# A layer of a hybrid decoder trunk: the second norm's parts as two streams, the residual rows on GpSimd's queue, the channel mixer's conditioning later

## The chip, the cores and the metric

The kernel runs on one core of a Trainium2 chip. The metric is the device time of one execution in microseconds; a shorter time is better. Times come from three runs of the kernel before, and one further execution was taken with the hardware profiler. TensorE (PE) does the matrix products, VectorE (DVE), ScalarE (ACT) and GpSimd (POOL) the elementwise work; SyncE (SP), ACT and POOL also issue DMA transfers, each in the order of its own instruction queue.

## The reference

One layer (depth 1) is applied to a prompt of 1024 tokens and to 8 sample groups of 8 tokens with the same weights, all in float32, with 1024 features:

```python
sh, sc, gt = ada_mod(c, w_ada_mix, b_ada_mix)          # silu(c) @ w + b, in three parts
h = rms_norm(x, norm_mix) * (1 + sc) + sh
pr, pp, pg = split(h @ w_in)
o_r = rwkv7_branch(pr, ...)                            # 512 columns, a scan over the tokens
o_p = pool_branch(pp, ...)                             # 512 columns, windowed means
g_r, g_p = split(sigmoid(pg))
merged = g_r * (o_r @ w_br_rwkv) + g_p * (o_p @ w_br_pool)
x = x + gt * (merged @ w_out)
sh, sc, gt = ada_mod(c, w_ada_mlp, b_ada_mlp)
h = rms_norm(x, norm_mlp) * (1 + sc) + sh
x = x + gt * (square(relu(h @ w_ff1)) @ w_ff2)         # hidden width 4096
y = rms_norm(x, norm_final)
```

The states of the branches are outputs too. The change touches the five lines from `merged` to the second `h`, and the way in which every `rms_norm` spreads its row of reciprocal roots.

## The kernel before

**Layout.** Features lie on the 128 partitions, tokens along a row: x is eight tiles of 128 x 1088 (1024 prompt and 64 sample tokens). Tokens are worked in three chunks of 364, 362 and 362; the first two, 726 tokens, are called part 0, the third part 1.

**Products.** A float32 product is made of three passes in a reduced type: hi by hi, hi by lo and lo by hi (`mm3`, L171 to L174), where hi is the rounded value and lo the rest. A weight tile of 128 x 512 is loaded by SP (L164), rounded by ACT (L167, `whi`), and its rest is made by DVE or, for every other tile, by POOL (L168, `wlo`). PSUM has four banks with the tag mm, two with w and two with wc; a bank comes free when its result has been read.

**Order.** PE's order is written out by `Pace.run` (L87): one stream of jobs (products) runs on, and generators (here `norm2` and `ada`) put their few matmuls between, after a given model time or when a condition holds. The scheduler of the tile framework orders the other engines. Every engine, and each DMA queue with it, works strictly in the order of its list.

**The stretch of the change** is `phase2` (L1222). It begins behind the jobs `op_job`, which multiply the pool branch's product into a gate row and save that row to DRAM (`d_th`, L1218 and L1220). Then:

- `or_job(m)`, eight jobs of 36 matmuls: two gate rows are loaded into tiles `t` and `u` (four buffers with the tag t) on ACT's queue (L1244, L1245); DVE multiplies the first with the RWKV branch's product (L1246); POOL adds the second, the *merge* (L1250); ACT and DVE split the sum into hi and lo (L1253, L1254).
- `x_load` (L1264): the eight rows of x, 544 KB each, come on ACT's queue into buffers of the tag hx (L1268).
- `out_job(m, i)`: 24 or 48 matmuls with `w_out` for part i, then the residual (L1433 on DVE; for the sample tokens L1436 on DVE into `rs` and L1438 on POOL).
- `norm2` (L1278), one generator: it waits for the whole conditioning, then for part 0 squares the rows (ACT, L1290), adds them (DVE, L1292), sums over partitions on PE (`stats`), makes the reciprocal roots (`rms`, L281: root L286, reciprocal L287, a copy that repeats each value 128 times L289, transposes on PE L155, ACT L302), modulates the eight rows (DVE L1303, L1305, L1307; ACT L1304, L1309; POOL L1310); and then all of it for part 1.
- `ada` (L1232): the conditioning of the channel mixer, 24 loads `hid` of 512 KB on SP (L249) and 48 narrow matmuls, in three groups: shift, scale and gate.
- `ff1_job` and `ff2_jobs`: the two products of the channel mixer. The first job for part i starts only when norm part i is done.

## Time and profile before

| what | value |
| --- | --- |
| median of 3 runs | 1761.83 us (1758.38 to 1764.14) |
| the profiled execution's own time | 1760.32 us |
| its span, first to last instruction | 1758.5 us |
| PE busy | 1688.9 us, 96% |
| DVE, ACT, POOL busy | 846.8, 546.0, 242.9 us |
| mean granted TensorE clock | 0.984 |
| stretch 786 to 857 us (merge jobs): PE busy, DMA share | 64.33 of 71.00 us, 0.90 |
| stretch 857 to 930 us (output, part 0) | 73.00 of 73.00 us, 0.44 |
| stretch 930 to 985 us (output, part 1, and norm) | 50.00 of 55.00 us, 0.28 |

A row of a timeline reads: start in us, length in us, engine, line, operation, output <- inputs and shapes, and in brackets the time that the engine stood idle before it, with what ended that time. A row of the chain of waits has the start, the length and the work that was waited for. A group's row has the count behind an x, then busy time, mean ns of one, and idle time before. DMA rows have the count, KB each and the median time from issue to landing.

### The profile page before, as it was taken

Reading aid. Unit: us, or ns where it says so; the run is one execution under the profiler, and the core shown is the slowest. Engines: PE = TensorE matmul, PEld = TensorE weight load, DVE = VectorE, ACT = ScalarE, POOL = GpSimd, SP = SyncE. Lnnn points to the kernel's source line nnn. Section 1 sums busy time; section 2 is a strip of 40 time slices with the busy share of each in tenths; the row PEclk is TensorE's granted clock in tenths of the full one; section 3 lists DMA queues with packets and bytes.
Section 4 is the critical chain, followed back from the end, with each engine's and each line's share of the span. In section 5 each row is a group of like instructions: output and inputs, shape, how many; then the busy total and the mean of one; then the engine's idle time right before and its main releaser. Section 6 shows DMA issues by size and latency. Waiting matters only on the chain.

```text
span 1758.5 us, 32538 instructions
## 1 busy us (share of the span) xinstructions
PE 1688.9 (96%) x13705; PEld 1582.7 (90%) x13705; DVE 846.8 (48%) x1546; ACT 546.0 (31%) x1100; POOL 242.9 (14%) x315
## 2 busy tenths in 40 slices
PE   5999999999999999998999999999999999999997
PEld 2989879887887898897889999999999999999996
DVE  5577475646663654344436643333333343323356
ACT  4443343334333433221224521213121222212132
POOL 0110111000000000003313511111111111111111
PEclk9999999999999999998999999999999999999999
DMA  8233314232413332849742211111111111111112
GB/s 336 83 126 119 124 65 138 83 104 88 131 42 127 97 120 72 315 156 356 257 150 78 85 61 42 49 43 43 48 42 48 44 43 48 42 49 43 43 42 103
DMA packets 80084, 179.61 MB, mean 102 GB/s; under 512 B 16481, under 2 KB 23137, under 8 KB 79937
## 3 DMA queue, kind: packets, MB, share of 16 engines
q1 hardware_dynamic: 72128, 156.66, 26.0%
q10 hardware_dynamic: 7664, 20.42, 3.4%
q8 instruction: 108, 1.77, 0.4%
q0 software_dynamic: 144, 0.44, 0.1%
q14 instruction: 40, 0.32, 0.1%
HBM read 138.64 MB, written 38.84 MB: 101 GB/s over the span
## 4 chain that ended last, share of the span: by engine, by line
PE 86%; DVE 5%; DMA 4%; ACT 2%; issue 1%; SPq 0%; DVEq 0%; ACTq 0%; POOL 0%
PE mm L148 58%; PE w L148 24%; PE wc L148 3%; DMA smp<-in_xT 1%; PE w L155 1%; DMA wt<-d_x 1%; DMA wraw<-in_w_in 1%; DVE wlo L168 1%; DMA d_th<-px 0%; DMA hx<-in_xT 0%; DMA t<-d_th 0%; DVE ma L1305 0%; DMA aw<-in_w_ada_mix 0%; DVE hx L1423 0%; DVE t L1303 0%
## 5 line engine op out<-in xcount | busy, mean ns | idle before, releaser
L148 PE MATMUL mm<-hx,whi 128*128 128x362 f32 (+2 forms) x2608 | 684.6, 344 | 9.0 <-DVE t L1246 6.5
L148 PEld LDWEIGHTS mm<-hx,whi 128*128 128x128 f32 x2608 | 459.0, 192 | 47.6 <-issue 28.4
L148 PE MATMUL mm<-hx,wlo 128*128 128x362 f32 (+3 forms) x1304 | 430.1, 330 | 1.8 <-DVE wlo L168 1.8
L167 ACT ACTIVATE whi<-wraw 128x512 fp32r<-128x512 f32 x246 | 155.0, 630 | 537.4 <-PE w L148 365.3
L148 PE MATMUL mm<-ma,whi 128*128 128x364 f32 (+1 forms) x1280 | 318.8, 330 | 0.0
L148 PEld LDWEIGHTS mm<-hx,wlo 128*128 128x128 f32 x1304 | 250.5, 192 | 2.3 <-DVE wlo L168 2.1
L148 PEld LDWEIGHTS mm<-ma,whi 128*128 128x128 f32 x1280 | 227.0, 189 | 6.7 <-issue 5.0
L168 DVE TENSOR_TENSOR wlo<-wraw,whi 128x512 fp32r<-128x512 f32 x157 | 111.9, 713 | 210.6 <-ACT whi L167 210.0
L148 PE MATMUL mm<-ma,wlo 128*128 128x364 f32 (+1 forms) x640 | 210.7, 329 | 0.0
L168 POOL TENSOR_TENSOR wlo<-wraw,whi 128x512 fp32r<-128x512 f32 x89 | 117.3, 1318 | 666.4 <-ACT whi L167 666.2
L1433 DVE SCALAR_TENSOR_TENSOR hx<-mm,aq,hx 128x364 f32<-128x364 f32 (+4 forms) x136 | 74.7, 587 | 206.4 <-PE mm L148 206.3
L148 PE MATMUL w<-mb,whi 128*128 128x362 f32 x640 | 159.0, 330 | 0.6 <-DVE rs L1436 0.6
L148 PEld LDWEIGHTS mm<-ma,wlo 128*128 128x128 f32 x640 | 120.9, 189 | 0.0
L148 PEld LDWEIGHTS w<-mb,whi 128*128 128x128 f32 x640 | 114.0, 191 | 0.8 <-issue 0.8
L1327 DVE TENSOR_TENSOR ft<-ft 128x362 f32<-128x362 f32 (+1 forms) x96 | 53.0, 576 | 127.4 <-ACT ft L1326 127.0
L148 PE MATMUL w<-mb,wlo 128*128 128x362 f32 x320 | 105.4, 329 | 1.3 <-DVE wlo L168 1.3
L148 PE MATMUL w<-hx,whi 128*128 128x362 f32 x416 | 103.5, 330 | 0.1
L148 PE MATMUL mm<-hid,whi 128*128 128x364 f32 (+4 forms) x304 | 75.3, 330 | 0.0
L148 PEld LDWEIGHTS w<-hx,whi 128*128 128x128 f32 x416 | 73.4, 190 | 1.2 <-issue 0.8
L1326 ACT ACTIVATE ft<-mm 128x364 f32<-128x364 f32 x64 | 29.3, 474 | 128.4 <-PE mm L148 128.3
L148 PE MATMUL w<-hx,wlo 128*128 128x362 f32 x208 | 67.8, 326 | 0.0
L148 PEld LDWEIGHTS w<-mb,wlo 128*128 128x128 f32 x320 | 61.1, 191 | 1.7 <-DVE wlo L168 1.7
(301 smaller groups left out, 2074.5 us busy)
## 6 DMA issues: line engine op xcount, KB each, us to landing
wraw<-in_w_ff SPq DMA_DIRECT2D x134, 256.0 KB, 2.6
wraw<-in_w_in SPq DMA_DIRECT2D x68, 256.0 KB, 3.0
hid<-in_w_ada_mlp SPq DMA_DIRECT2D x24, 512.0 KB, 5.1
d_th<-px SPq DMA_DIRECT2D x22, 544.0 KB, 3.1
wt<-d_x SPq DMA_DIRECT2D x20, 544.0 KB, 4.3
t<-d_th ACTq DMA_DIRECT2D x16, 544.0 KB, 6.7
aw<-in_w_ada_mix SPq DMA_DIRECT2D x16, 512.0 KB, 7.1
wraw<-in_w_out SPq DMA_DIRECT2D x32, 256.0 KB, 2.7
```

The source lines that it names most:

```text
L148: return self.nc.tensor.matmul(out, lhsT, rhs, **kw)
L155: self.nc.tensor.transpose(out, in_, ident)
L167: nc.scalar.activation(hi, raw, AF.Copy)
L168: (nc.gpsimd if n % 2 and n >= self.solo else nc.vector).tensor_tensor(lo, raw, hi.bitcast(F32), op=ALU.subtract)
L1326: nc.scalar.activation(t[:, :n], ps[:, :n], AF.Relu)
L1327: nc.vector.tensor_tensor(t[:, :n], t[:, :n], t[:, :n], op=ALU.mult)
L1433: nc.vector.scalar_tensor_tensor(x[:, c0:c0 + m], ps[:, :m], gt[:, 0:1], x[:, c0:c0 + m], op0=ALU.mult, op1=ALU.add)
```

## The change

- **x loads.** `x_load` goes. Each `or_job` ends with a one-column copy on POOL from its merged row into a buffer for x (`behind`), and a load of one row of x into that buffer on POOL's queue. The copy makes the load stand behind the merge.
- **Conditioning.** `ada` starts when the fifth or-job's place in the order is reached (`("or", 8)` is set by job 4). Its first four tiles are tied to merged rows by the same copy. Its third group, the gates, waits until norm part 1 is done, and no longer holds up the norm.
- **Norm.** `norm2(i)` is one generator for each part. The squares and sums of a part no longer wait for the conditioning, and those of part 1 no longer for part 0's modulation; they have an own sum (`acc2`) and use the tiles `ft`. Part 1's modulation waits for part 0's.
- **`rms`.** The copy that repeats each reciprocal 128 times goes; PE's transposes read the single column as a broadcast.

```diff
@@ -278,21 +278,22 @@
             m = len(blocks) if first and i == 0 else 1
             self.mm(po[:, i:i + m], t[:, b:b + 128], self.kc("one0")[:, :m], start=first and i == 0, stop=last and i == len(blocks) - 1)
 
-    def rms(self, po, col, blocks, out, pool):
+    def rms(self, po, col, blocks, out):
 
         nc = self.nc
         k = len(blocks)
         r = self.cp.tile([P, 16], F32, tag="rt", bufs=2, name=self.nm("rt"))[:, :k]
         nc.scalar.activation(r, po[:, col:col + k], AF.Sqrt, bias=self.eps[:, 0:1], scale=1.0 / D)
         nc.vector.reciprocal(r, r)
-        R = self.row(pool, "R", 1, w=9 * 128).rearrange("p (b j) -> p b j", j=128)
-        nc.vector.tensor_copy(R[:, :k, :], r.unsqueeze(2).to_broadcast([P, k, 128]))
         yield 2000
         for i in range(0, k, 4):
             m = min(4, k - i)
             ps = self.ps("wc")
             for j in range(m):
-                self.tr(ps[:, j * 128:(j + 1) * 128], R[:, i + j, :], self.kc("ident"))
+                self.tr(ps[:, j * 128:(j + 1) * 128], r[:, i + j:i + j + 1].to_broadcast([P, 128]), self.kc("ident"))
+            self.rps = ps
+            if out is None:
+                return
             for j in range(m):
                 if j + 1 < m and blocks[i + j + 1] == blocks[i + j] + 128:
                     continue
@@ -394,7 +395,7 @@
                 nc.vector.scalar_tensor_tensor(lo[:, pr], h, sh, hi[:, pr].bitcast(F32), op0=ALU.add, op1=ALU.subtract)
                 nc.vector.tensor_tensor(lo[:, sa], smp[:, kb], hi[:, sa].bitcast(F32), op=ALU.subtract)
 
-        self.pace.run(iter(()), [part(0, (0, 3500, 0, 0), 1000), self.rms(po, 0, blocks, rb, st)])
+        self.pace.run(iter(()), [part(0, (0, 3500, 0, 0), 1000), self.rms(po, 0, blocks, rb)])
         load(1)
 
         def rest():
@@ -1229,11 +1230,26 @@
         orr = self.orr
         mg = [[], []]
 
+        def behind(x):
+
+            nc.gpsimd.tensor_copy(x[:, 0:1], self.mark[:, 0:1])
+            return x
+
         def ada():
-            asb = self.row(p, "R", 1, w=9 * 128)[:, :512]
+            asb = p.tile([P, 512], F32, name="asb2")
+            yield lambda: ("or", 8) in self.done
+            first = 4 * [behind]
+
+            def tile():
+                t = self.row(p, "hid", 4)[:, :1024]
+                return first.pop()(t) if first else t
+
             for g in range(3):
-                yield from self.ada_part("w_ada_mlp", g, lambda: self.row(p, "hid", 4)[:, :1024], asb, self.aq, "b_mlp", (8 * g, 8 * g + 4), 7000, 3000, 15000 if g == 0 else 0)
-            self.done.add("ada")
+                if g == 2:
+
+                    self.done.add("ada")
+                    yield lambda: ("h2", 1) in self.done
+                yield from self.ada_part("w_ada_mlp", g, tile, asb, self.aq, "b_mlp", (8 * g, 8 * g + 4), 6500, 2500, 9000 if g == 0 else 0)
 
         def or_job(m):
             S = {}
@@ -1254,6 +1270,10 @@
                     nc.vector.tensor_tensor(lo[i], t[:, s], hi[i].bitcast(F32), op=ALU.subtract)
                 mg[0].append(hi)
                 mg[1].append(lo)
+                self.mark = t
+                self.xr.append(HX(F32))
+                nc.gpsimd.dma_start(behind(self.xr[m]), io["xT"][m])
+                self.done.add(("or", m + 4))
 
             return Job([io["w_br"][m][:, 0:512]], begin, after=after, xs=lambda: orr, tags=TG)
 
@@ -1261,12 +1281,7 @@
         g2 = self.cp.tile([P, 8, 9], F32, name="g2")
         self.xr = []
 
-        def x_load():
-            nc.vector.tensor_scalar(gt, self.am[:, 16:24, :], 0.5, None, op0=ALU.mult)
-            for m in range(8):
-                self.xr.append(HX(F32))
-                nc.scalar.dma_start(self.xr[m], io["xT"][m])
-            yield
+        nc.vector.tensor_scalar(gt, self.am[:, 16:24, :], 0.5, None, op0=ALU.mult)
 
         def out_job(m, i):
             ch = (CH[:2], CH[2:])[i]
@@ -1275,41 +1290,48 @@
 
         fh, fl = [[None, None] for _ in range(8)], [[None, None] for _ in range(8)]
 
-        def norm2():
+        def norm2(i):
+            a, b = ((0, CUT), (CUT, NT))[i]
+            bl = [x for c0, n in (CH[:2], CH[2:])[i] for x in self.blocks(c0 - a, n)]
+            if i:
+                acc, sq = p.tile([P, NT - CUT], F32, name="acc2"), lambda: p.tile([P, 364], F32, tag="ft", bufs=2, name=self.nm("ft"))[:, :NT - CUT]
+            else:
+                acc, sq = T()[:, :CUT], lambda: T()[:, :CUT]
+            for m in range(8):
+                yield lambda: ("out", m, i) in self.done
+                t = sq() if m else acc
+                nc.scalar.activation(t, self.xr[m][:, a:b], AF.Square)
+                if 0 < m < 7:
+                    nc.vector.tensor_tensor(acc, acc, t, op=ALU.add)
+                if m > 5:
+                    yield 3500
+                    po = self.ps("wc") if m == 6 else po
+                    self.stats(po, acc if m == 6 else t, bl, m == 6, m == 7)
             yield lambda: "ada" in self.done
-            self.mod_scale(g2, self.aq, "norm_mlp")
-            rb = T()
-            for i, ch in enumerate((CH[:2], CH[2:])):
-                a, b = ch[0][0], ch[-1][0] + ch[-1][1]
-                bl = [x for c0, n in ch for x in self.blocks(c0, n)]
-                po = self.ps("wc")
-                acc = T()
-                for m in range(8):
-                    yield lambda: ("out", m, i) in self.done
-                    t = T() if m else acc
-                    nc.scalar.activation(t[:, a:b], self.xr[m][:, a:b], AF.Square)
-                    if 0 < m < 7:
-                        nc.vector.tensor_tensor(acc[:, a:b], acc[:, a:b], t[:, a:b], op=ALU.add)
-                    if m > 5:
-                        yield 3500
-                        self.stats(po, acc if m == 6 else t, bl, m == 6, m == 7)
-                yield from self.rms(po, 0, bl, rb, p)
-                for kb in range(8):
...
-                self.done.add(("h2", i))
+            if i:
+                r = acc
+            else:
+                self.mod_scale(g2, self.aq, "norm_mlp")
+                r = T()[:, :CUT]
+            yield from self.rms(po, 0, bl, r)
+            if i:
+                yield lambda: ("h2", 0) in self.done
+            for kb in range(8):
...
+            self.done.add(("h2", i))
 
         hid = {}
 
@@ -1348,7 +1370,6 @@
         order = []
         for m in range(8):
             order += U(or_job(m))
-        order += [(x_load, 0)]
         for i in range(2):
             for m in range(8):
                 order += U(out_job(m, i))
@@ -1366,7 +1387,7 @@
                 if j == 0 and grp:
                     for j2 in ff2_jobs(grp - 1):
                         order += U(j2)
-        self.pace.run(self.stream(None, order), [norm2(), ada()])
+        self.pace.run(self.stream(None, order), [norm2(0), norm2(1), ada()])
 
 
         w = []
@@ -1413,7 +1434,7 @@
                     if m > 5:
                         yield 2500
                         self.stats(po, acc if m == 6 else t, bl, m == 6, m == 7)
-                yield from self.rms(po, 0, bl, rb[:, c0:c0 + n], p)
+                yield from self.rms(po, 0, bl, rb[:, c0:c0 + n])
                 for m in (7, 6, 0, 1, 2, 3, 4, 5):
                     x = self.xr[m][:, c0:c0 + n]
                     if m > 5 and ci == 2:
```

In the two places marked in `norm2`, the loop over the eight rows is the same before and after (it reads `r` in place of a slice of `rb`).

The change moves instructions at three places that matter here. First, ACT's list at the start of `phase2`, before: `hx<-in_xT` are the x loads, `t_8646` and `t_8647` the gate rows of the first or-job.

```order
L167 ACTIVATE whi_8618<-wraw_8616 128x512
L1268 DMA hx_9175<-in_xT 128x1088
L1035 ACTIVATE hx_8549<-wt_7132 128x576
L1268 DMA hx_9177<-in_xT 128x1088
L1268 DMA hx_9179<-in_xT 128x1088
L1268 DMA hx_9181<-in_xT 128x1088
L1268 DMA hx_9183<-in_xT 128x1088
L1268 DMA hx_9185<-in_xT 128x1088
L167 ACTIVATE whi_8624<-wraw_8622 128x512
L1268 DMA hx_9187<-in_xT 128x1088
L1268 DMA hx_9189<-in_xT 128x1088
L167 ACTIVATE whi_8630<-wraw_8628 128x512
```

The same place of ACT's list in the changed program, up to the gate rows of the second or-job:

```order
L167 ACTIVATE whi_8617<-wraw_8615 128x512
L1036 ACTIVATE hx_8547<-wt_7130 128x576
L167 ACTIVATE whi_8623<-wraw_8621 128x512
L167 ACTIVATE whi_8629<-wraw_8627 128x512
L1260 DMA t_8642<-d_th_90 128x1088
L1261 DMA t_8643<-d_th_98 128x1088
L167 ACTIVATE whi_8635<-wraw_8633 128x512
L1260 DMA t_8706<-d_th_91 128x1088
L1261 DMA t_8707<-d_th_99 128x1088
```

The eight x loads no longer stand ahead of the gate rows on ACT. Second, POOL's list over the first or-jobs in the changed program; before, the merges and the `wlo` rows stand here alone.

```order
L1266 TENSOR_TENSOR t_8642<-t_8642,t_8643 128x1088
L1235 COPY hx_8703<-t_8642 128x1
L1275 DMA hx_8703<-in_xT 128x1088
L1266 TENSOR_TENSOR t_8706<-t_8706,t_8707 128x1088
L168 TENSOR_TENSOR wlo_8752<-wraw_8749,whi_8751 128x512
L1235 COPY hx_8767<-t_8706 128x1
L1275 DMA hx_8767<-in_xT 128x1088
```

Each merge is now followed by its copy and one x load. Third, DVE's list in the norm, before: from the fourth row's residual of part 1 (`hx_9181`) over modulation rows (`t`, `ma`), to the fifth row's (`hx_9183`).

```order
L1307 TENSOR_TENSOR t_9997<-hx_9181,t_9756 128x726
L1305 SCALAR_TENSOR_TENSOR ma_9975<-t_9976,aq,ma_9974 128x726
L1433 SCALAR_TENSOR_TENSOR hx_9181<-w_9967,gt_8614,hx_9181 128x298
L1303 SCALAR_TENSOR_TENSOR t_10013<-hx_9183,g_8615,t_9756 128x726
L1436 TENSOR_TENSOR rs_10024<-w_9967,gt_8614 128x64
L168 TENSOR_TENSOR wlo_9989<-wraw_9986,whi_9988 128x512
L1303 SCALAR_TENSOR_TENSOR t_10039<-hx_9185,g_8615,t_9756 128x726
L1433 SCALAR_TENSOR_TENSOR hx_9183<-w_10027,gt_8614,hx_9183 128x298
```

The same place in the changed program, where `acc_8640` is the sum of part 1's squares and `hx_8895` and `hx_8959` are the fourth and fifth row:

```order
L1329 TENSOR_TENSOR t_9961<-hx_8895,t_9830 128x726
L1327 SCALAR_TENSOR_TENSOR ma_9931<-t_9932,aq,ma_9930 128x726
L168 TENSOR_TENSOR wlo_9972<-wraw_9969,whi_9971 128x512
L1325 SCALAR_TENSOR_TENSOR t_9983<-hx_8959,g_8613,t_9830 128x726
L1305 TENSOR_TENSOR acc_8640<-acc_8640,ft_9950 128x362
L1454 SCALAR_TENSOR_TENSOR hx_8895<-w_9946,gt_8612,hx_8895 128x298
L1457 TENSOR_TENSOR rs_10000<-w_9946,gt_8612 128x64
L1325 SCALAR_TENSOR_TENSOR t_10009<-hx_9030,g_8613,t_9830 128x726
```

An add of squares stands between modulation rows, and the weight rest (`wlo`) ahead of the fourth row's residual instead of behind it.

More of the change, by code (lines that the diff above doesn't have):

```diff
@@ L1276, in phase2 @@
         fh, fl = [[None, None] for _ in range(8)], [[None, None] for _ in range(8)]
-        def norm2():
-            yield lambda: "ada" in self.done
-            self.mod_scale(g2, self.aq, "norm_mlp")
-            rb = T()
-            for i, ch in enumerate((CH[:2], CH[2:])):
-                a, b = ch[0][0], ch[-1][0] + ch[-1][1]
-                bl = [x for c0, n in ch for x in self.blocks(c0, n)]
-                po = self.ps("wc")
-                acc = T()
-                for m in range(8):
-                    yield lambda: ("out", m, i) in self.done
-                    t = T() if m else acc
-                    nc.scalar.activation(t[:, a:b], self.xr[m][:, a:b], AF.Square)
-                    if 0 < m < 7:
-                        nc.vector.tensor_tensor(acc[:, a:b], acc[:, a:b], t[:, a:b], op=ALU.add)
-                    if m > 5:
-                        yield 3500
-                        self.stats(po, acc if m == 6 else t, bl, m == 6, m == 7)
-                yield from self.rms(po, 0, bl, rb, p)
-                for kb in range(8):
-                    hi, lo = fh[kb][i], fl[kb][i] = MG(i), MG(i)
-                    h = T()[:, a:b]
-                    x, r, sh = self.xr[kb][:, a:b], rb[:, a:b], self.aq[:, kb, 0:1]
-                    if i == 0 and kb % 4 < 3:
-                        nc.vector.scalar_tensor_tensor(h, x, g2[:, kb, 0:1], r, op0=ALU.mult, op1=ALU.mult)
-                        nc.scalar.activation(hi, h, AF.Identity, bias=sh)
-                        nc.vector.scalar_tensor_tensor(lo, h, sh, hi.bitcast(F32), op0=ALU.add, op1=ALU.subtract)
-                    else:
-                        nc.vector.tensor_tensor(h, x, r, op=ALU.mult)
-                        self.modulate(h, h, g2, self.aq, kb, a, b - a, a)
-                        nc.scalar.activation(hi, h, AF.Copy)
-                        (nc.gpsimd if kb % 4 == 3 else nc.vector).tensor_tensor(lo, h, hi.bitcast(F32), op=ALU.subtract)
-                    yield 1000
-                self.done.add(("h2", i))
@@ new lines, in norm2 @@
+        def norm2(i):
[15 more added lines that the diff above has]
+                    self.stats(po, acc if m == 6 else t, bl, m == 6, m == 7)
+            yield lambda: "ada" in self.done
+            if i:
[7 more added lines that the diff above has]
+            for kb in range(8):
+                hi, lo = fh[kb][i], fl[kb][i] = MG(i), MG(i)
+                h = T()[:, a:b]
+                x, sh = self.xr[kb][:, a:b], self.aq[:, kb, 0:1]
+                if i == 0 and kb % 4 < 3:
+                    nc.vector.scalar_tensor_tensor(h, x, g2[:, kb, 0:1], r, op0=ALU.mult, op1=ALU.mult)
+                    nc.scalar.activation(hi, h, AF.Identity, bias=sh)
+                    nc.vector.scalar_tensor_tensor(lo, h, sh, hi.bitcast(F32), op0=ALU.add, op1=ALU.subtract)
+                else:
+                    nc.vector.tensor_tensor(h, x, r, op=ALU.mult)
+                    self.modulate(h, h, g2, self.aq, kb, a, b - a, a)
+                    nc.scalar.activation(hi, h, AF.Copy)
+                    (nc.gpsimd if kb % 4 == 3 else nc.vector).tensor_tensor(lo, h, hi.bitcast(F32), op=ALU.subtract)
+                yield 1000
+            self.done.add(("h2", i))
```

## The prediction

> **What bounds the kernel now.** I read the totals first, then PE's own waits in time order, then the chain of waits and the clock around each stop. The page's first lines:
>
> ```profile
> span 1758.5 us, 32538 instructions
> PE 1688.9 (96%) x13705; PEld 1582.7 (90%) x13705; DVE 846.8 (48%) x1546; ACT 546.0 (31%) x1100; POOL 242.9 (14%) x315
> ```
>
> TensorE is the bound, so only its stops and its slow stretches can be won. The change touches the merge, the output product and the second norm (about 786 to 985 us). In PE's timeline there I find three stops:
>
> ```profile
> 811.89 0.95 PE L148 MATMUL mm<-hx,whi 128*128 128x364 f32 x2 [6.48 <-DVE t L1246]
> 955.61 0.57 PE L148 MATMUL w<-mb,whi 128*128 128x362 f32 x2 [0.56 <-DVE rs L1436]
> 957.53 0.43 PE L148 MATMUL w<-mb,wlo 128*128 128x362 f32 x1 [1.35 <-DVE wlo L168]
> 974.51 0.94 PE L148 MATMUL wc<-kct,t 128*128 128x3 f32 x6 [3.09 <-DVE t L1292]
> ```
>
> The bracket is PE's idle time and who ended it. Each stop is followed by a stretch at a lower clock; the view of stretches (length, busy time of PE, PEld, DVE, ACT, POOL, then PE's granted clock, DMA share, GB/s):
>
> ```profile
> 812.00:818.00 6.00, 6.00 (x20) 6.00 (x21) 2.30 (x6) 1.09 (x2) 2.50 (x1) 0.50 1.04 401
> 957.50:961.50 4.00, 3.97 (x14) 3.97 (x15) 4.00 (x7) 2.49 (x4) 1.59 (x3) 0.57 0.23 70
> 974.50:979.00 4.50, 4.49 (x19) 4.49 (x20) 0.56 (x1) 0.79 (x2) 1.27 (x1) 0.62 0.34 113
> 985.00:1190.00 205.00, 205.00 (x1241) 205.00 (x1240) 85.31 (x152) 55.78 (x111) 44.34 (x54) 1.00 0.16 52
> ```
>
> The last row shows PE without a stop at clock 1.00, so each slow stretch is charged to the stop ahead of it: length times (1 - clock). Stop A: 6.48 + 6.0 x 0.50 = 9.5 us. Stop B: 0.56 + 1.35 + 4.0 x 0.43 = 3.6. Stop C: 3.09 + 4.5 x 0.38 = 4.8. That is 17.9 us, the most that the change can win here.
>
> **Stop A: the x loads leave ACT's queue.** The chain of waits around A, in order of time (start, length):
>
> ```profile
> 789.39 7.11 DMA hx<-in_xT
> 796.58 7.69 DMA d_th<-px
> 804.40 6.72 DMA t<-d_th
> ```
>
> Before, a save of the gate product cannot be issued until one of the x loads has landed; the first t load waits for that save, because it writes the save's old buffer; and VectorE's gating, which frees the PSUM bank that PE wants, waits for t. SyncE's waits and ACT's row say the same, and VectorE's row shows that the data of the last save were there early:
>
> ```profile
> SPq L1220 <- DMA hx<-in_xT: 6.3, 1, 6.3
> 804.37 0.63 ACT L167 ACTIVATE whi<-wraw 128x512 fp32r<-128x512 f32 x1 [10.28 <-DMA d_th<-px]
> 792.58 1.52 DVE L1218 SCALAR_TENSOR_TENSOR px<-px,mm 128x364 f32<-128x364 f32 x3 [1.79 <-PE mm L148]
> ```
>
> The product is complete at 792.58 + 1.52 = 794.1. Landing times (KB, median us), the first two rows of the stretch 786 to 805, the last of the whole page:
>
> ```profile
> hx<-in_xT ACTq DMA_DIRECT2D x8, 544.0 KB, 8.9
> d_th<-px SPq DMA_DIRECT2D x2, 544.0 KB, 6.8
> d_th<-px SPq DMA_DIRECT2D x22, 544.0 KB, 3.1
> ```
>
> In the changed program no x load stands on ACT, and the first one on POOL stands behind the first merge. So the save is issued at 794.2 and lands at 797.3 (3.1) or at latest 801.0 (6.8). One weight copy (0.63) is ahead of the t load, which takes from 3.1 (the same size with the x loads away) to 6.72: t is there between 801 and 804.6, in the worst case at 808.4. Gating to PE's start took 811.89 - 811.21, the end of the t load plus 0.1: 0.7 to 0.8. PE wants the bank at 811.89 - 6.48 = 805.4. In the middle cases the bank is free by then; in the worst one 809.2, 3.8 us late, with 3.8 / 6.48 x 3.0 = 1.8 of slow clock. So A gives between 9.5 - 5.6 = 3.9 and 9.5. I take 9.5: the eight loads that made these transfers slow are gone from that stretch.
>
> **Where the x loads go.** They stand on POOL, each behind one merge and a one-column copy that ties it to that merge. POOL's groups in the merge stage, and its rows near the start, the only DMAs it issues before:
>
> ```profile
> L168 POOL TENSOR_TENSOR wlo<-wraw,whi 128x512 fp32r<-128x512 f32 x22 | 30.0, 1364 | 102.1 <-ACT whi L167 102.0
> L1250 POOL TENSOR_TENSOR t<-t,t 128x1088 f32<-128x1088 f32 x8 | 21.4, 2673 | 28.0 <-DMA t<-d_th 16.6 <-PE mm L148 7.2 <-DVE t L1246 3.0
> L427 POOL COPY px<-sst 128x8 f32<-128x8 f32 x2 | 0.9, 460 | 5.6 <-DMA sst<-in_sst 5.6
> 1.99 0.54 POOL L1115 DMA_DIRECT2D kct<-in_kc  x1
> kct<-in_kc POOLq DMA_DIRECT2D x1, 315.5 KB, 6.6
> 856.80 5.96 PE mm L148 x36
> ```
>
> One merge job is 36 matmuls of PE, 5.96 us. POOL's share of a job: merge 2.67, half a weight remainder 0.68, one and a half copies at 0.46 = 0.69, issue 0.54: 4.58 of 5.96. It fits with 1.38 to spare, so I price it at nothing; the cover is that margin, and an issue that holds POOL for more than 0.54 + 1.38 = 1.92 us makes it late, eight times. The upper bound for an issue is the landing itself, 6.6. No issue of POOL's in this trace stands beside a busy VectorE, so the price is not shown here.
>
> The Trainium skill, "SBUF — State Buffer", section "SBUF: two separate sides", speaks against the change at this place: a DMA issued by GpSimd needs descriptors that GpSimd writes, and a VectorE instruction in a two-port mode locks it out; it gives about 620 ns alone and 3100 ns beside such an instruction. By that figure, an estimate from that page, the loss would be 8 x (3.1 - 1.92) = 9.4 us and the time about 1757; no run so far shows it, and it stands below as a rival priced from rows.
>
> The residual reads x only in the output stage, after the last merge job, so an x load has tens of us to land.
>
> **The mixer's conditioning.** Its 24 loads of 512 KB stay on SyncE, but now begin behind the fourth or so merge; the last third, the gates, is computed during the first product of the channel mixer.
>
> ```profile
> hid<-in_w_ada_mlp SPq DMA_DIRECT2D x24, 512.0 KB, 5.1
> ```
>
> The same matmuls run, elsewhere. The one tight place is the second pair of tiles: by the order it is issued about 1.4 us before the last merge job ends, and PE wants it about 5.0 after. 5.1 - 6.4 leaves 1.3 us of slack at the median; a landing of 8.9, like the x loads', would cost 2.5. I charge 0.5 (0 to 2.5). The gates are ready 66 matmuls (11 us at 5.96 us per 36) before the second product begins: nothing.
>
> **Stops B and C: the second norm as two streams.** VectorE's timeline, from the start of the norm's first part to the end of C:
>
> ```profile
> 940.49 0.56 DVE L289 COPY R<-rt 128x768 f32<-128x768 f32 x1
> ...
> 944.83 2.75 DVE L1303 SCALAR_TENSOR_TENSOR t<-hx,g,t 128x726 f32<-128x726 f32 x3 [1.62 <-ACT t L302]
> ...
> 955.25 0.21 DVE L1436 TENSOR_TENSOR rs<-w,gt 128x64 f32<-128x64 f32 x1
> 955.39 2.09 DVE L168 TENSOR_TENSOR wlo<-wraw,whi 128x512 fp32r<-128x512 f32 x1
> 957.40 1.02 DVE L1303 SCALAR_TENSOR_TENSOR t<-hx,g,t 128x726 f32<-128x726 f32 x1
> ...
> 963.27 0.90 DVE L1307 TENSOR_TENSOR t<-hx,t 128x726 f32<-128x726 f32 x1
> 964.10 0.52 DVE L1433 SCALAR_TENSOR_TENSOR hx<-w,gt,hx 128x298 f32<-128x298 f32 x1
> 964.54 0.21 DVE L1436 TENSOR_TENSOR rs<-w,gt 128x64 f32<-128x64 f32 x1
> 964.67 0.96 DVE L1305 SCALAR_TENSOR_TENSOR ma<-t,aq,ma 128x726 fp32r<-128x726 f32 x1
> 965.76 0.69 DVE L168 TENSOR_TENSOR wlo<-wraw,whi 128x512 fp32r<-128x512 f32 x1
> ...
> 967.56 0.53 DVE L1292 TENSOR_TENSOR t<-t,t 128x362 f32<-128x362 f32 x1
> ...
> 971.78 2.67 DVE L1292 TENSOR_TENSOR t<-t,t 128x362 f32<-128x362 f32 x3
> ```
>
> VectorE is the late engine: it modulates part 0, serves part 1's residuals, and only then adds part 1's squares, whose last three (971.78 + 2.67 = 974.45) release C. The change adds no work here; it moves. (1) Part 0's transposes stand 6 matmuls earlier (1.0 us), and the 0.56 copy ahead of them goes, so the modulation starts 0.6 to 1.0 us sooner against PE; I take 0.8. (2) Two of part 1's adds now stand ahead of the fourth row's gating (rs), and the weight remainder that made B's 1.35 stands two operations ahead of it. From the modulation's start to that rs the new list is 2.75 + 1.02 + 3 x 0.96 + 0.90 + 2 x (0.69 + 0.53 + 0.52 + 0.21) = 11.45, less about 0.07 by which each of 13 starts before its predecessor's end (964.10 + 0.52 against 964.54, 964.54 + 0.21 against 964.67): 10.5. Operations here also run long, as 2.09 against 0.69 shows, so 10.5 to 11.7. PE wanted the bank at 955.61 - 0.56 = 955.05, 10.2 after 944.83; now 11.0. Stall 0 to 0.7, I take 0.3. The next remainder, still behind two modulations, I put at 0.7 late (0 to 1.4, B's own size being the bound). (3) The last add stands right behind the last-but-one residual, not behind three others: 3.09 goes to between 0 and 3.09 less the two adds that no longer follow (1.1), 2.0; I take 0.8. Idle left: 1.8 of 5.0. The clock lost there was 3.4; at the same share per idle us it would be 1.2, but B's 1.91 us of idle alone drew 1.7, so I keep 1.6. B and C give 8.4 - 3.4 = 5.0, between 0 and 8.4.
>
> The Trainium skill, "TensorE: Matmul & The Clock Gate", Part 1, puts the slow clock only after an idle window of about 3.4 us. The rows above disagree: 0.57 for 4.0 us after 1.91 us of idle in two pieces. The measurement decides; by the rule the 1.6 would not be lost, and the forecast would be 1745.9.
>
> **The copy of the reciprocal, elsewhere.** It goes from all norms; only the last one lies on the path to the end:
>
> ```profile
> 1749.65 0.30 DVE R L289
> ```
>
> This row of the chain of waits is the 0.3 that I count. The first norm's copy lies behind input loads: nothing. PE's transposes now read one column broadcast; no row shows such a read. The load as it is:
>
> ```profile
> L155 PEld LDWEIGHTS wc<-kct,R x27: 138/142/231, 24.6 to 1750.1; 128*128 128x128 f32 x27
> ```
>
> If it took twice or half as long (27 x 0.14), that would be +3.8 or -1.9 at most; it overlaps the matmul before it, so I take 0.
>
> **Sum.** -9.5 (A) - 5.0 (B, C) - 0.3 + 0.5 = -14.3. Against this execution's own 1760.32 us: 1746.0. The median of the runs is 1.5 above that execution, so 1747.5; I say 1747.
>
> **Rivals.**
> 1. *Only A goes.* VectorE's work in the norm is the same, and B and C merely change their place: -9.5 - 0.3 + 0.5 = -9.3, 1752.5. For it: VectorE is busy without gap from 944.83 on. Against: the adds that release C are moved ahead.
> 2. *All three go* and the conditioning costs nothing: -17.9 - 0.3, 1743.6. Against: the budget of 10.5 to 11.7 against 11.0.
> 3. *POOL's issues wait for VectorE* (the mechanism that the skill's page tells). An issue that is held for two VectorE operations in a row of 1.0 to 1.3 us takes 0.54 + 2.6 = 3.1: 8 x (3.1 - 1.92) = 9.4 lost, -4.9, 1757. Held for one it takes 1.8 and costs nothing.
> 4. *A stays:* the save turns out to wait for another transfer. Then -5.0 - 0.3 + 0.5 = -4.8, 1757. Against: the row that names the x load.
> 5. *Slower:* each issue holds POOL until its transfer has landed, 6.6 us, so POOL sets the merge stage: 8 x (6.6 - 1.92) = 37 lost, +23, about 1785. It decides from 1.92 + 14.3 / 8 = 3.7 us per issue. Against: at 1.99 the issue took 0.54 while its transfer took 6.6.
>
> **How the numbers follow.** My forecast 0.46, rival 1 0.18, rival 2 0.12, rival 3 0.09, rival 4 0.08, rival 5 or another mishap as dear 0.07. Range 1740 to 1758: all three stops with the transposes' gain below, rivals 3 and 4 above. The forecast's own range is 1742 to 1752. 0.3% is 5.3 us, about what a measurement of this kernel tells from no change. Forecast and rivals 1 and 2 are faster (0.76); rivals 3 and 4 lie on the bound, 1757 against 1756.5, a third of them faster (0.05): faster 0.81, same 0.12, slower 0.07.
>
> **What would show it.** In the new profile: no stop of PE at the second merge job, and the merge stage at clock 1.00 (A); the save issued within 1 us of its product; x loads on POOL with issues under 1.9 us; PE's wait on the square adds under 1 us and under 2 us together with B's. I am wrong if POOL's merges start late with the t loads landed, if PE waits for conditioning tiles, or if the waits on VectorE add up to 5 us as before.

## The result, and the profile after

The changed kernel took 1755.55 us (median of 18 runs, 1750.53 to 1759.69) against 1764.6 us for the kernel before (median of 18 runs beside it, 1758.38 to 1771.96): ratio 0.9949, interval 0.9936 to 0.9963, 9 us faster. The forecast was 1747, 14.3 us faster.

The two profiled executions show less: spans of 1758.5 and 1757.5 us. They already differ by 4 us ahead of the change, as this PE row at one and the same place of the program shows, first of the kernel before, then of the changed one (start, length, work, idle time and its end):

```profile
702.80 0.60 PE L148 MATMUL mm<-hx,whi 128*128 128x362 f32 x2 [2.03 <-ACT px L464]
```

```profile
706.97 0.60 PE L148 MATMUL mm<-hx,whi 128*128 128x362 f32 x2 [2.03 <-ACT px L465]
```

In the fourteen profiles of this study that row stands between 701.71 and 709.46 us, with nearly the same work ahead of it. So the profiles are compared below from this common point to the third norm's first sums, also in PE's timeline:

```profile
1732.94 0.83 PE L148 MATMUL wc<-kct,t 128*128 128x3 f32 x6 [0.76 <-DVE t L1412]
```

```profile
1731.64 0.83 PE L148 MATMUL wc<-kct,t 128*128 128x3 f32 x6 [0.79 <-DVE t L1433]
```

That is 1030.1 us before and 1024.7 after, 5.5 us less. PE's stops of the changed kernel in the stretch of the change, the answer to the three stops of before:

```profile
846.79 1.05 PE L148 MATMUL wc<-hid,sT 128*32 128x512 f32 x4 [2.04 <-DMA hid<-in_w_ada_mlp]
856.83 1.05 PE L148 MATMUL wc<-hid,sT 128*32 128x512 f32 x4 [1.35 <-DMA hid<-in_w_ada_mlp]
951.48 0.57 PE L148 MATMUL w<-mb,whi 128*128 128x362 f32 x2 [2.07 <-DVE rs L1457]
960.12 0.57 PE L148 MATMUL w<-mb,whi 128*128 128x362 f32 x2 [0.40 <-ACT t L334]
961.51 0.43 PE L148 MATMUL w<-mb,wlo 128*128 128x362 f32 x1 [0.82 <-DVE wlo L168]
975.40 0.54 PE L155 MATMUL wc<-kct,rt 128*128 128x128 f32 x3 [0.38 <-DVE rt L287]
```

Stop A, 6.48 us at the second merge job, is gone; two stops on the conditioning's tiles have come, 31 and 41 us later by the distance from the common point. Each costs more than its bracket. A row of the kernel before and the row ahead of the first stop after show why:

```profile
833.43 1.07 PE L148 MATMUL wc<-hid,sT 128*32 128x512 f32 x8
```

```profile
843.70 1.05 PE L148 MATMUL wc<-hid,sT 128*32 128x512 f32 x4
```

Eight matmul records on a pair of tiles take 1.07 us together. With only one tile there, four of them take 1.05, and the other four another 1.05 later: a pair used half by half costs 1.05 us over the idle time. The two stops are 2.04 + 1.35 + 2 x 1.05 = 5.5 us, with no slow clock behind them. The stretches of both kernels, before first (length, busy PE, PEld, DVE, ACT, POOL, PE's clock, DMA share, GB/s):

```profile
790.00:870.00 80.00, 73.33 (x432) 67.44 (x431) 34.19 (x53) 18.83 (x33) 30.67 (x15) 0.94 0.87 316
930.00:985.00 55.00, 50.00 (x295) 49.05 (x294) 34.76 (x51) 26.28 (x45) 22.70 (x19) 0.94 0.28 88
```

```profile
790.00:870.00 80.00, 76.61 (x455) 71.61 (x454) 40.61 (x62) 19.96 (x33) 38.40 (x35) 1.00 0.82 296
930.00:985.00 55.00, 50.89 (x306) 48.54 (x305) 39.67 (x61) 31.54 (x59) 29.84 (x30) 1.00 0.30 92
```

GpSimd's part went as forecast. The issues of the x loads, from POOL's timeline and the line's own view:

```profile
830.59 3.08 POOL L1250 TENSOR_TENSOR t<-t,t 128x1088 f32<-128x1088 f32 x1 [0.29 <-DVE t L1246]
```

```profile
841.37 0.56 POOL L1275 DMA_DIRECT2D hx<-in_xT  x1 [0.32 <-POOL hx L1235]
846.66 2.50 POOL L1266 TENSOR_TENSOR t<-t,t 128x1088 f32<-128x1088 f32 x1 [4.72 <-DMA t<-d_th]
```

```profile
L1275 POOL DMA_DIRECT2D hx<-in_xT x8: 551/561/570, 810.1 to 856.6; - x8
DMA to landing us min/median/max: 6.0/6.9/9.0
```

The first row is one of the merges before, for comparison. Eight issues took 0.55 to 0.57 us each, beside a VectorE that was about half busy (40.61 of 80 us), and the merge behind one waits for its gate row, not for POOL. The Trainium skill, "SBUF — State Buffer", section "SBUF: two separate sides", gives 3.1 us in place of 0.62 for a DMA that GpSimd issues beside a VectorE instruction in a two-port mode. None of the eight issues was held for so long; which of VectorE's instructions beside them are of that kind the trace does not say.

### The profile page after: what moved, and what is told of

It is laid out like the page before. It is cut to its first block, busy times and chain, and to the rows that moved or that the text cites. A ratio compares the mean times of both kernels' runs of the same rounds, so it can differ in the third digit from the quotient of the medians.

```text
span 1757.5 us, 32572 instructions
## 1 busy us (share of the span) xinstructions
PE 1692.8 (96%) x13705; PEld 1583.7 (90%) x13705; DVE 845.0 (48%) x1540; ACT 546.1 (31%) x1100; POOL 255.1 (15%) x335
## 4 chain that ended last, share of the span: by engine, by line
PE 86%; DMA 4%; DVE 4%; ACT 2%; issue 2%; POOL 1%; SPq 0%; DVEq 0%; ACTq 0%; POOLq 0%
PE mm L148 58%; PE w L148 24%; PE wc L148 4%; DMA t<-d_th 1%; DMA smp<-in_xT 1%; PE w L155 1%; POOL t L1266 1%; DMA aw<-in_w_ada_mix 1%; DMA wraw<-in_w_in 1%; DMA hid<-in_w_ada_mlp 0%; ACT whi L167 0%; DVE hx L1444 0%; DMA wraw<-in_w_ff 0%; POOL wlo L168 0%; DVE wlo L168 0%
## 5 line engine op out<-in xcount | busy, mean ns | idle before, releaser
L1459 POOL TENSOR_TENSOR hx<-hx,rs 128x64 f32<-128x64 f32 x72 | 38.6, 537 | 176.8 <-DVE rs L1457 176.6
```

Of the source, the lines that this page charges most:

```text
L1459: nc.gpsimd.tensor_tensor(x[:, NPR:NT], x[:, NPR:NT], t, op=ALU.add)
```

## The experiments

All times are ratios to the kernel before, run beside each. "Common point" is the measure above; before it is 1030.1 us. It and the idle times are of one execution each; how far they can be trusted stands at the last experiment. Idle times are sums of PE's brackets of 0.25 us and more, in the merge stage and in the norm's stage; slow clock and half-used pairs come on top.

| kernel | idle, merge | idle, norm | common point | ratio (interval) |
| --- | --- | --- | --- | --- |
| before | 6.48 | 5.00 | 1030.1 | 1 |
| changed | 3.39 | 3.67 | 1024.7 | 0.9949 (0.9936 to 0.9963) |
| x loads alone | 6.70 | 5.46 | 1031.2 | 1.0010 (0.9996 to 1.0025) |
| norm alone | 6.64 | 3.48 | 1030.8 | 0.9999 (0.9986 to 1.0012) |
| conditioning alone | 4.37 | 3.67 | 1026.3 | 0.9961 (0.9948 to 0.9974) |
| changed, conditioning early | 6.30 | 3.66 | 1029.8 | 0.9984 (0.9972 to 0.9996) |
| changed, x loads at the start | 3.65 | 3.58 | 1025.4 | 0.9974 (0.9962 to 0.9987) |
| changed, later use | 4.80 | 4.14 | 1028.7 | 0.9967 (0.9954 to 0.9980) |
| changed, tiles untied | 5.10 | 4.13 | 1029.9 | 0.9974 (0.9960 to 0.9987) |
| x loads later | 1.52 | 2.66 | 1022.5 | 0.9951 (0.9937 to 0.9966) |
| x loads later, later use | 8.35 | 2.91 | 1032.2 | 0.9995 (0.9982 to 1.0007) |
| x loads later, tie earlier | 1.97 | 3.59 | 1021.9 | 0.9956 (0.9938 to 0.9973) |
| more transfers | 12.16 | 2.91 | 1042.4 | 1.0037 (1.0022 to 1.0051) |
| x loads later, tie earlier, shifted | 3.23 | 4.38 | 1025.1 | 0.9944 (0.9924 to 0.9963) |

The first theory was the forecast's own: A went with the x loads, B and C with the norm, and the tiles' two stops are a separate fault of the conditioning's new place. Its rival: the merge stage needs a certain amount of DMA time, and what is loaded in it only decides who waits.

**Use the tiles later.**

```diff
-                ... (8 * g, 8 * g + 4), 6500, 2500, 9000 if g == 0 else 0)
+                ... (8 * g, 8 * g + 4), 6500, 2500, 15000 if g == 0 else 0)
```

> The changed kernel with one number altered: the conditioning's first matmuls stand 6 us (model time) later on PE behind its first loads (15000 in place of 9000); the loads' ties are kept. Theory (the 5 us missing from the forecast are the two stops of PE on conditioning tiles, each with a pair of tiles used half by half): both stops go, PE waits under 0.5 us for conditioning tiles, and the time falls by 4 to 5.5 us below the changed kernel's 1755.6, ratio to the kernel before about 0.9920. Rival (the stage lacks DMA bandwidth, so a later use only moves the stop to the next tiles or to the gate rows): the stops' sum stays above 2.5 us and the ratio at 0.9940 or above.

Measured: 0.9967, not below the changed kernel. The first tile stop went, but 2.96 us of the second remained, and two waits for the last merged row came (1.30 and 0.54). The rival's case.

**Load the tiles without a tie.**

```diff
-            first = 4 * [behind]
+            first = []
```

> The changed kernel with the four one-column copies on the conditioning's first tiles taken away, so that these loads wait for nothing but their place on SyncE. Theory 1 (the tie makes the tiles late): SyncE issues the first pair at about 830 in place of 834.6, and the second pair up to 2 us earlier; the stops shrink from 3.4 to under 1 us, the time by 3 to 5 us. Theory 2 (DMA is full, with gate rows, x rows and conditioning in the same 30 us): the earlier tiles land as slowly (9 us and more), gate rows get later by as much, and the time changes by less than 2 us.

Measured: 0.9974, some 4.4 us above the changed kernel, where theory 2 had under 2. No tile stop is left; instead PE waits for the last merged row. PE's timeline:

```profile
830.65 0.57 PE L148 MATMUL mm<-hx,whi 128*128 128x364 f32 x2 [0.57 <-DVE t L1262]
856.70 0.67 PE L148 MATMUL mm<-ma,whi 128*128 128x364 f32 x1 [4.25 <-ACT ma L1269]
857.65 0.67 PE L148 MATMUL mm<-ma,whi 128*128 128x364 f32 x1 [0.28 <-DVE ma L1270]
```

Theory 1 fell. Theory 2 had the way of it, but not the size: the gate rows lost more than the tiles gained. Without the ties the four first tiles stand on SyncE right behind the saves, far ahead of their use, as they did before the change.

**The x loads alone, on the kernel before.**

```diff
+                self.mark = t
+                self.xr.append(HX(F32))
+                nc.gpsimd.dma_start(behind(self.xr[m]), io["xT"][m])
...
-        order += [(x_load, 0)]
```

> The kernel before with only the x loads moved: each on GpSimd's queue behind a merge and its one-column copy. Conditioning, norm and the reciprocal's copy are as before. Theory (the x loads alone made stop A): the 6.5 us stop and the slow clock behind it go, 9.5 us, ratio to the kernel before 0.9946. Rival (with the x loads gone, the first conditioning loads, which SyncE then issues at the same place, take their part and delay the first gate row): PE still waits 2 us or more for the first gating, gain 6 us or less, ratio 0.9966 or above.

Measured: 1.0010, no gain at all: within the rival's number, but not at its place. Stop A at the second job is gone, and this stands in PE's timeline:

```profile
835.08 0.57 PE L148 MATMUL mm<-hx,whi 128*128 128x364 f32 x2 [2.07 <-DVE t L1251]
863.00 0.67 PE L148 MATMUL mm<-ma,whi 128*128 128x364 f32 x1 [4.35 <-ACT ma L1258]
863.95 0.67 PE L148 MATMUL mm<-ma,whi 128*128 128x364 f32 x1 [0.28 <-DVE ma L1259]
```

6.70 us of waits for gate rows in place of 6.48. The stop has moved to the stage's end; in the stretch 812 to 865 its gate rows took 7.7 us to land (6.2 before), its conditioning tiles 8.3 (6.7 before) and its x rows 8.5. In four stretches of 15 us from 790 on, the DMA share before was 0.98, 1.02, 0.86 and 0.96; with the x loads moved, at the same distances from the common point, it is 0.69, 0.96, 1.02 and 1.01. The full part of the stage has moved with the loads, and PE's waits with it.

**The norm alone, on the kernel before.** `norm2` as in the change, with the copy of the reciprocal kept:

```diff
-        self.pace.run(self.stream(None, order), [norm2(), ada()])
+        self.pace.run(self.stream(None, order), [norm2(0), norm2(1), ada()])
```

> The kernel before with only the second norm as two generators, with an own sum for part 1; x loads, conditioning and the reciprocal's copy as before (that copy's tile is made six blocks wide to fit). Theory (stop C was the adds' place in VectorE's list): C under 1 us, B about as before, 3 to 5 us gained, ratio to the kernel before 0.9975. Rival (VectorE's work is the same and the stop only moves ahead): B grows by what C loses, within 1 us of the kernel before, ratio 0.9994 or above.

Measured: 0.9999. C fell from 3.09 to 0.85 us, B grew to 0.57 + 2.06. The time is the rival's, but B grew by 0.7 us only: 1.5 us of idle went, and the slow clock of the stage stayed at 0.94. What took the 1.5 us back stands at the last experiment.

**The conditioning alone, on the kernel before.** `ada` as in the change (fifth merge, ties, gates behind the norm); x loads, norm and copy as before:

```diff
+            yield lambda: ("or", 8) in self.done
+            first = 4 * [behind]
...
+                    self.done.add("ada")
+                    yield lambda: ("h2", 1) in self.done
```

> The kernel before with only the conditioning moved as in the change (begins behind the fifth merge, its gates behind the norm); x loads on ACT's queue at the start, the norm as one generator and the reciprocal's copy as before. Theory (the merge stage has a fixed need of DMA time; whoever is loaded there delays something else): stop A stays at about 6.5 us with its slow clock, since the x loads make it alone; the conditioning tiles meet a freer DMA and PE waits under 1 us for them; the time is within 2 us of the kernel before, ratio 0.999 to 1.001. Rival (the early conditioning loads, which fill the same 20 us, were the greater part of A): A falls below 4 us, ratio 0.9975 or below.

Measured: 0.9961, most of the whole change's gain. The rival held. PE's timeline:

```profile
811.08 0.95 PE L148 MATMUL mm<-hx,whi 128*128 128x364 f32 x2 [3.62 <-DVE t L1261]
855.37 1.05 PE L148 MATMUL wc<-hid,sT 128*32 128x512 f32 x4 [0.41 <-DMA hid<-in_w_ada_mlp]
856.76 1.05 PE L148 MATMUL wc<-hid,sT 128*32 128x512 f32 x4 [0.34 <-DMA hid<-in_w_ada_mlp]
957.42 0.67 PE L148 MATMUL w<-mb,wlo 128*128 128x362 f32 x1 [3.67 <-DVE wlo L168]
```

A shrinks by 2.9 us although every x load stands where it stood: what has gone from there are three conditioning loads that SyncE issued from 798.13 before. And C is gone without the norm in two streams; that the norm waits for two groups of the conditioning in place of three, and so starts sooner, would explain it, but no run took the groups apart. So not all of this gain is the merge stage's: there idle fell from 6.48 to 4.37 us and the clock rose from 0.94 to 0.98, in the norm's stage idle fell from 5.00 to 3.67 and the clock rose from 0.94 to 0.97.

**The change with the conditioning back in its old place.** `ada` as before; all else as changed.

> The changed kernel with the conditioning put back where it was (begins at once, all three groups ahead of the norm); x loads on GpSimd's queue behind merges, the norm in two streams, no reciprocal copy. Theory (fixed need of DMA time): the stop that A was comes back at a later merge job and at the first output job, 6 to 10 us with slow clock as with the x loads alone moved, and only the norm's part is left, ratio 0.998 to 1.000. Rival (the three parts add up each by itself, and the x loads alone read too high by chance): the ratio stays near the changed kernel's, 0.996 or below.

Measured: 0.9984, in the theory's range, near its faster end; 6.30 us of waits for gate rows, at the same two places as with the x loads alone (1.44, then 4.35 and 0.51).

**The change with the x loads back at the start, on ACT's queue.**

```diff
-                nc.gpsimd.dma_start(behind(self.xr[m]), io["xT"][m])
...
+        order += [(x_load, 0)]
```

> The changed kernel with the x loads put back on ACT's queue at the start of the stage; conditioning, norm and the missing copy as in the change. Theory (the conditioning's move carries the gain, the x loads' move only shifts the stop): stop A at about 3.6 us as with the conditioning alone moved, no stop on tiles over 1 us, ratio 0.995 to 0.997. Rival (the x loads' move is worth the 9.5 us of stop A once the conditioning is out of the way): ratio 0.998 or above.

Measured: 0.9974, between the two expectations; A at 3.65 us and no tile stop, as the theory had it. Moving the x loads is worth 0.0025 in the ratio by the medians and 0.8 us by the common point; not nothing, and far from 9.5 us. The runs with and without the norm in two streams (0.9974 and 0.9961) show no gain of that part on top of the conditioning's move; 1.5 us of their difference are the buffers' addresses of the last experiment.

**Fewer x loads in the merge stage.**

```diff
-                self.xr.append(HX(F32))
-                nc.gpsimd.dma_start(behind(self.xr[m]), io["xT"][m])
+                for k in ((), (), (), (), (0,), (1,), (2, 3), (4, 5, 6, 7))[m]:
+                    self.xr.append(HX(F32))
+                    nc.gpsimd.dma_start(behind(self.xr[k]), io["xT"][k])
```

> The changed kernel with the x loads later: x rows 0 to 3 behind the fifth to seventh merge (one, one and two), rows 4 to 7 behind the eighth, so that four to six of the eight 544 KB loads leave the merge stage for the output stage, where DMA is about half used. Theory (fixed need of DMA time in the merge stage): the stops of the merge stage, 3.4 us of idle and two pairs of tiles used half by half, go to under 1 us, and the time falls 3 to 5.5 us below the changed kernel, ratio about 0.9925. Rival (the tie of the tiles to the merges, not the bandwidth, makes them late): both stops stay above 2.5 us in sum, ratio 0.994 or above.

Measured: the tile stops fell from 3.39 to 0.85 + 0.67, the common point by 2.2 us, the ratio not at all (0.9951). The stops are the theory's, the time is the rival's, so this run decides nothing: that fewer transfers in the stage shorten the time is not shown.

**And the tiles used later.** 12000 in place of 9000 in the same line as above.

> The run with the later x loads, and the conditioning's first matmuls 3 us (model time) later behind their loads (12000 in place of 9000). Theory (fixed need of DMA time): with the stage relieved the later use takes away what is left of the tiles' stops, 0 to 1.5 us better than the later x loads alone, ratio 0.991 to 0.9925, where the later use alone had made the changed kernel no faster. Rival (a later use pushes the tiles' stop to the end of the stage whatever else is loaded): PE waits over 2 us at the last merge job or the first output job, ratio 0.994 or above.

Measured: 0.9995; the rival's number, for a reason of its own. PE's timeline, and SyncE's:

```profile
862.67 1.92 PE L148 MATMUL wc<-hid,sT 128*32 128x512 f32 x4 [6.41 <-DMA hid<-in_w_ada_mlp]
865.28 1.91 PE L148 MATMUL wc<-hid,sT 128*32 128x512 f32 x4 [0.69 <-DMA hid<-in_w_ada_mlp]
```

```profile
836.40 14.47 SPq L164 DMA_DIRECT2D wraw<-in_w_out  x3
850.96 0.86 SPq L249 DMA_DIRECT2D hid<-in_w_ada_mlp  x2
853.88 0.33 SPq L164 DMA_DIRECT2D wraw<-in_w_out  x1
855.17 1.00 SPq L249 DMA_DIRECT2D hid<-in_w_ada_mlp  x2
```

In this program's list of SyncE the third pair of tiles, which must wait until PE has used the first, stands ahead of the second pair. So the second is issued only from 855.17, and PE has it whole at 865.28, 10.1 us later. With 9000 (x loads later) the pairs stand in their order. In the changed kernel's list the first load of the third pair also stands ahead of the second pair.

**The tie one job earlier.** On top of the later x loads:

```diff
-            yield lambda: ("or", 8) in self.done
+            yield lambda: ("or", 7) in self.done
```

with 15000, so that PE uses the tiles at the changed kernel's place.

> The run with the later x loads, and the conditioning's first two tiles tied to the fourth merge in place of the fifth; PE uses them at the same place as in the changed kernel. Theory (fixed need of DMA time in the merge stage, and the tiles' stops are what is left of it): the first tiles' stop goes, 0.85 us and the 1.05 us of the pair used half by half, the second stays at 0.7 and 1.05, so about 2 us better than the later x loads alone, ratio about 0.994. Rival (nothing is left to gain here, tiles loaded earlier delay gate rows by as much): gate rows make PE wait 1 us or more in the merge stage, ratio 0.995 or above.

Measured: 0.9956 with two stops of 0.98 and 0.99; inconclusive, neither theory's numbers.

**More transfers.** Eight rows of x are also written to the gate rows' places in DRAM, where nobody reads them.

```diff
                 nc.gpsimd.dma_start(behind(self.xr[m]), io["xT"][m])
+                nc.gpsimd.dma_start(self.d_th[m], io["xT"][m])
```

> The changed kernel with eight more transfers of 544 KB, from x in DRAM to the gate rows' places in DRAM, each issued by GpSimd behind the load of that job's gate row; nobody reads them. It adds work and takes none away. Theory (the merge stage has a fixed need of DMA time): 4.4 MB more, at the 400 GB/s that the stage moves when full some 11 us, come back as PE's waits for gate rows and conditioning tiles in the merge stage, with slow clock: 8 to 15 us slower than the changed kernel, ratio about 1.001. Rival (the waits come from the order and the ties, DMA has room): the time stays within 2 us of the changed kernel, ratio 0.996 or below.

Measured: 1.0037; 17.7 us longer from the common point than the changed kernel, 0.0088 in the ratio, about 15.5 us. PE's timeline:

```profile
840.46 0.94 PE L148 MATMUL mm<-hx,whi 128*128 128x364 f32 x2 [3.54 <-DVE t L1262]
848.26 1.05 PE L148 MATMUL wc<-hid,sT 128*32 128x512 f32 x4 [0.64 <-DMA hid<-in_w_ada_mlp]
852.61 1.88 PE L148 MATMUL wc<-hid,sT 128*32 128x512 f32 x4 [3.30 <-DMA hid<-in_w_ada_mlp]
865.49 1.11 PE L148 MATMUL wc<-hid,sT 128*32 128x512 f32 x4 [3.58 <-DMA hid<-in_w_ada_mlp]
867.71 1.92 PE L148 MATMUL wc<-hid,sT 128*32 128x512 f32 x4 [1.10 <-DMA hid<-in_w_ada_mlp]
```

8.8 us more idle in the merge stage, on gate rows and tiles alike, and more slow clock and half-used pairs. The dose acts in the direction and slightly above the size that a stage short of DMA time would give. With the x loads alone, which takes nothing out of the stage, and the conditioning alone, which does, this is the ground on which the first theory was given up. The reverse did not show: with the later x loads, fewer transfers in the stage, the ratio stayed where it was.

**The buffers behind the norm's sum, 64 bytes further.** On top of the later x loads and the earlier tie. From the first to the last residual of 364 columns in the channel mixer, the kernel before, then the changed kernel, then this run (DVE's timeline, two rows each):

```profile
1042.19 1.10 DVE L1433 SCALAR_TENSOR_TENSOR hx<-mm,aq,hx 128x364 f32<-128x364 f32 x2 [0.43 <-PE mm L148]
...
1655.70 1.10 DVE L1433 SCALAR_TENSOR_TENSOR hx<-mm,aq,hx 128x364 f32<-128x364 f32 x2 [3.68 <-PE mm L148]
```

```profile
1039.45 1.10 DVE L1454 SCALAR_TENSOR_TENSOR hx<-mm,aq,hx 128x364 f32<-128x364 f32 x2 [0.44 <-PE mm L148]
...
1654.44 1.10 DVE L1454 SCALAR_TENSOR_TENSOR hx<-mm,aq,hx 128x364 f32<-128x364 f32 x2 [3.69 <-PE mm L148]
```

```profile
1039.92 1.10 DVE L1455 SCALAR_TENSOR_TENSOR hx<-mm,aq,hx 128x364 f32<-128x364 f32 x2 [0.43 <-PE mm L148]
...
1653.43 1.10 DVE L1455 SCALAR_TENSOR_TENSOR hx<-mm,aq,hx 128x364 f32<-128x364 f32 x2 [3.68 <-PE mm L148]
```

```diff
-                acc, sq = p.tile([P, NT - CUT], F32, name="acc2"), ...
+                acc, sq = p.tile([P, 384], F32, name="acc2")[:, :NT - CUT], ...
```

> The run with the later x loads and the earlier tie, with one edit: the sum tile of part 1 is 384 columns wide in place of 362, of which 362 are used as before, so that every buffer allocated behind it in SBUF begins 64 bytes later; no instruction is added or moved. It is for 1.5 us that all runs with the norm in two streams lose evenly in the channel mixer, where nothing waits: from the first to the last residual of 364 columns the kernel before, the x loads alone and the conditioning alone took 613.51 us, the changed kernel, the norm alone and the run without the x move 614.99. Theory (the addresses: in the three kernels at 613.51 the buffers behind begin at 64 modulo 128 bytes, in the three at 614.99 at 0): 613.5 us in this stretch. Rival (the order of instructions in the norm leaves some other state): 615.0 as before. The time itself is within 2 us of the run without the edit, ratio 0.993 to 0.996.

Measured: 613.51, 614.99, 613.51 us. One edit of an address, no instruction moved, and the 1.48 us are back to the hundredth. The ratio is 0.9944, the best of the study but within the changed kernel's interval. Beside this gain the same program stood 3.2 us later from the common point than the run without the edit (1025.1 against 1021.9), with tile stops of 3.23 in place of 1.97: one execution differs from another by about 5 us in these stages, so differences of 2 or 3 us in that column, the later x loads' among them, are not shown, nor are differences of 1 us in a single profile's stops. The 5.5 us of the whole change stand only just outside; its ratio of 18 runs is the better measure.

## Why the prediction was right, and where it was not

The kernel became faster, as forecast, and its time lies in the forecast's range: 9.0 of 14.3 us came. The sum behind it was right only in part. One of its own signs of being wrong came true in the profile, that PE waits for conditioning tiles, and the waits of B and C add up to 3.67 us, not to under 2.

- **A, -9.5.** The stop went, with its slow clock: the chain through x load, save and gate row was read rightly, and the save landed in time. The step that failed is the sentence that the eight loads "are gone from that stretch" as if that were enough: they stay in the merge stage, whose DMA share was 0.87 over 80 us before and is 0.82 after. By themselves they won nothing (1.0010). Of the stage's 9.5 us the whole change won 4.0 (9.5 - 5.5), and what made the difference is that the conditioning's loads left the front of the stage: the conditioning's move alone won 0.0039 of the 0.0051, though some of it in the norm's stage.
- **The conditioning, +0.5 (0 to 2.5).** This is the mis-sized term: 5.5 us. I weighed the second pair only. The first pair, issued at 834.61, also came late, its two tiles 8.9 and 11.6 us after their issue; the second hung on a merge at 846.66 that waited for its gate row, and landed in 6.7 us, not 5.1. What I had not priced at all is the pair used half by half, 1.05 us each time.
- **B and C, -5.0.** The size holds: 8.4 before, 3.67 of idle and no slow clock after, -4.8. That is luck in part: idle was twice the 1.8 us of the forecast, and of the 1.6 us of slow clock nothing came, while the run with the x loads later had 2.66 us of idle and clock 0.97 in the same stretch. The place doesn't hold: B is 2.07 + 0.40 + 0.82, C 0.38. The modulation did start sooner against PE, and by more than the 0.8 us of the forecast: PE wanted the fourth row's bank 951.48 - 2.07 - 937.91 = 11.5 us after that start, against 10.2 before. What failed is VectorE's budget of 10.5 to 11.7 us up to that row's `rs`: it took 951.13 + 0.21 - 937.91 = 13.4. The first three modulation rows took 3.52 us in place of 2.75, and the two adds that the change puts into the list 1.62 and 1.60, not 0.53 each (VectorE's timeline of the changed kernel):

```profile
937.91 3.52 DVE L1325 SCALAR_TENSOR_TENSOR t<-hx,g,t 128x726 f32<-128x726 f32 x3 [0.32 <-ACT t L303]
...
942.85 1.62 DVE L1305 TENSOR_TENSOR acc<-acc,ft 128x362 f32<-128x362 f32 x1
...
949.17 1.60 DVE L1305 TENSOR_TENSOR acc<-acc,ft 128x362 f32<-128x362 f32 x1
950.69 0.52 DVE L1454 SCALAR_TENSOR_TENSOR hx<-w,gt,hx 128x298 f32<-128x298 f32 x1
951.13 0.21 DVE L1457 TENSOR_TENSOR rs<-w,gt 128x64 f32<-128x64 f32 x1
```

  And the cause holds only in part: the two streams alone took 1.5 us of idle, which the addresses took back (0.9999), while the conditioning alone also left 3.67 us of idle, with the norm as it was.
- **The copy, -0.3.** PE's wait for the last transposes went from 0.97 to 0.64 us, 0.33.
- **POOL at nothing, rivals 3 and 5.** Right: 0.56 us per issue. **Rival 4** fell, and **rival 1**, only A goes, was near in size (-9.3 against the -9.0 measured) for a wrong reason.
- **Not in the sum:** +1.5 us by the buffers' addresses.

The account from the common point is -4.0 - 4.8 + 1.5 = -7.3 us, the profiles show -5.5, the medians -9.0 with an interval of some 2.5 us to each side (0.9936 to 0.9963). The 1.8 us between account and profile are open; so is the rest to the medians, but it is no more than one execution differs from another.

## What to carry to other kernels

A stop that one transfer releases is worth its length only if the stage has DMA time to spare: ask how many bytes the whole stage must move, and whether the change takes any out of it. Here moving the loads whose stop was visible was worth little, and moving the conditioning, whose loads were issued 35 us ahead of their use (798 and 833), was worth most, which only taking the change apart could show. Where a group of small matmuls works on two tiles at once, price a late tile with the second pass too.

## What the runs showed that was not expected

- The addresses of buffers in SBUF changed PE's pace by 0.24%: 613.51 or 614.99 us for the same stretch, in all 14 profiles one of the two to 0.01 us. By the addresses in the programs it was the shorter where the buffers, the hidden tiles among them, began at 64 modulo 128 bytes, and the longer where they began at 0; which of the moved buffers matter, the modulated rows, the hidden tiles or the small ones beside them, was not tried.
- One-column ties on four early loads were worth 0.0025 of the ratio (untied 0.9974, tied 0.9949, their intervals just overlapping): without them SyncE issued three of the four from 795.78 on, into the stage's front, with them the first at 834.61.
- The clock behind a stop is not a function of the stop: B's 2.07 us left the norm's stage at clock 1.00 in the changed kernel, while with the x loads later 2.06 us at the same place were followed by clock 0.50 from 949.5 to 952.5. The Trainium skill, "TensorE: Matmul & The Clock Gate", Part 1, says the window that the clock follows runs freely; these two agree with that.
